# Attention's key and query reorderings cut into pieces of 512 columns, and two buffers of the last input restore moved

## The chip, the cores and the metric

The program runs on one core of one Trainium2 chip. What is measured is the device time of one execution in microseconds, here the median of three runs. A profile comes from one more execution, taken by the hardware profiler.

## The reference

One layer of a hybrid block on 2048 tokens of width 1024. The input x is normalised (RMSNorm) and multiplied by one matrix of 9216 columns, nine slices of 1024: for branch A u, v and a gate; for branch B queries, keys, values and a gate; and two merge gates.

Branch A applies gelu to u and v, normalises v, mixes the positions of each chunk of 128 tokens with a lower-triangular 128x128 matrix for each of 8 channel groups, and multiplies by u and by the SiLU of its gate.

Branch B is causal attention with 16 heads of 64 channels in three patterns of distance (dilations 1, 4 and 16; pattern numbers p = 0, 1, 2). In the pattern of dilation d a query sees up to 129 keys whose positions differ by multiples of d, with a penalty linear in distance:

```python
s = jnp.einsum('bhrnqd,bhrnkd->bhrnqk', qb, kw) * (Dh ** -0.5)
s = s - slopes[None, :, None, None, None, None] * (dist * dilation).astype(jnp.float32)
```

The three outputs are combined by their softmax denominators and multiplied by the SiLU of the gate of B. Then merged = g_a * (y_a @ w_proj_a) + g_b * (y_b @ w_proj_b), x + merged @ w_out, and a last RMSNorm.

## The kernel before

Matrix products that need float32 accuracy are made of three products of rounded parts (`mm3`, line 97): a matrix is split into a high part and the rest (`split_w`, `split_X`), and hi*hi, hi*lo and lo*hi are summed. A product of 128x1024 by 1024x512 is so 24 matmuls of 512 columns.

**First part, two halves of the sequence.** Each half has two quarters of 512 tokens (qd). `make_h` loads the transposed input, scales it by the norm's statistics `rsbc` (made in `stats`, line 155, held in pool `tp`) and splits it into tiles X. Most slices are multiplied with a seven-product scheme (`unit_S`, `unit_SR`, one level of Strassen), whose sums of quarters stand in the tiles T1, T2, T3 (pool `tp`) and T4. T4 takes the place of the first four chunks of the second quarter's X. So at the end of each half `restore` (line 216) loads these four chunks again, scales them with `rsbc` (line 151, on VectorE) and splits them (lines 144 and 145). It does this through the buffers of tag `ld`, of which there are three.

**Stage change.** When the second half ends, pools `tp`, `wr` and `cp` are closed, and what opens then, `wp` (weight blocks of 128 columns: `wraw`, `whi`, `wlo`) and `at` (everything of the attention), lies in the same memory. A tile of the new pools can be written only when the old tiles in its bytes have been read for the last time.

**Window (lines 747 to 825).** The attention of 16 heads runs as 192 groups (head, pattern in the order 2, 1, 0, group g of 4 blocks of 128 queries). Step j issues the scores of group j (`stage_s`), the transposes of the probabilities of group j-2 (`stage_t`), and the weighted sum of group j-3 (`stage_o`); in between, dense products (`fill`: the rest of the gates for the second half, then the projection of branch A) are put in by a fixed ratio, 8 matmuls at a time. The order on TensorE is that of the program text (`issue_after`); on the other engines, and in the DMA queue of SyncE, a scheduler orders instructions at compile time, and can put one that is ready ahead of earlier ones in the text.

**Reordering.** For patterns 1 and 2 the keys (a high part KH and a low part KL, fp16, 2048 columns) are copied into block order (`permute`, line 594), for pattern 2 the queries as well. Per head these are five copies of 128x2048: for pattern 2 QP on ScalarE, KHP and KLP on VectorE; for pattern 1 KHP on VectorE and KLP on ScalarE. In the text, the generator `permuted` is started at group 0 of the pattern ahead, and advanced one copy per step (line 803). QP has one buffer; KHP and KLP have two, which patterns 2 and 1 use in turn.

**Last part** (`final`): projection of branch B, merge, output projection, norm.

Of the kernel before, what the change touches and what calls it, by code (L numbers as in the profile page):

```python
# [9 lines left out]
F32 = mybir.dt.float32  # L10
F32R = mybir.dt.float32r
F16 = mybir.dt.float16
AF = mybir.ActivationFunctionType
ALU = mybir.AluOpType
AX = mybir.AxisListType

P = 128
D = 1024
T = 2048
KC = D // P  # L20
# [7 lines left out]
class Prog:  # L28
# [126 lines left out]
    def stats(self, hp, qd):  # L155
        nc, io = self.nc, self.io
        ss = hp.tile([P, 4], F32, name="ss", tag="ss")
        for b in range(4):
            xr = hp.tile([P, D], F32, name="xr", tag="xr", bufs=2)
            t0 = 512 * qd + P * b  # L160
            nc.sync.dma_start(out=xr, in_=io["x"][t0:t0 + P])
            nc.scalar.activation(xr, xr, AF.Square, accum_out=ss[:, b:b + 1])
        rs = hp.tile([P, 4], F32, name="rs", tag="rs")
        self.rsqrt_mean(rs, ss, 4)
        ps = self.pt()
        for i in range(4):
            nc.tensor.matmul(ps[:, i * P:(i + 1) * P], rs[:, i:i + 1].broadcast_to([P, P]), self.ident,
                             start=True, stop=True)
        bc = self.tp.tile([P, 512], F32, name="rsbc", tag=f"rsbc{qd % 2}")
        nc.scalar.copy(bc, ps)  # L170
        self.bc[qd % 2] = bc

# [43 lines left out]
    def restore(self, X, qd, ks=range(4)):  # L216

        for k in ks:
            X[1][k] = [self.xp.tile([P, 512], F32R, name=f"X1_{k}_{p}", tag=f"X1_{k}_{p}") for p in range(2)]
            self.split_X(X[1], k, self.h_chunk(self.wk, "ld", 3, qd, k))  # L220

    def wraw(self, w, c0):
        raw = self.wr.tile([P, KC, 256], F32, name="wraw2", tag="wraw2", bufs=2)
        self.nc.sync.dma_start(out=raw, in_=w[:, c0:c0 + 256].rearrange("(k p) n -> p k n", p=P))
        return raw
# [242 lines left out]

    def ev_av(self, hf):
        nc = self.nc  # L470
        self.ssv = self.tp.tile([P, 8, 4], F32, name="ssv", tag="ssv")

        def ev(wb, np_, ps):
            t = ps.rearrange("p (c n) -> p c n", c=2)
            nc.scalar.activation(t, t, AF.Gelu_apprx_tanh)
            j = self.wk.tile([P, 512], F32, name="junk", tag="t5")[:, :256]
            for c in range(2):
                n = 2 * np_ + c
                nc.scalar.activation(j, t[:, c], AF.Square, accum_out=self.ssv[:, n, wb:wb + 1])
            nc.sync.dma_start(out=self.av_d[hf][256 * np_:256 * np_ + 256, wb * 256:wb * 256 + 256]  # L480
                              .rearrange("(c p) d -> p c d", c=2), in_=t)
        return ev
# [111 lines left out]
    def permute(self, at, copy, t, name, p, bufs):  # L594

        r = at.tile([P, T], F16, name=name, tag=name, bufs=bufs)
        if p == 1:
            copy(r.rearrange("p (q n a) -> p q n a", q=4, n=4), t.rearrange("p (n a q) -> p q n a", q=4, n=4))
        else:
            copy(r.rearrange("p (q a) -> p q a", q=16), t.rearrange("p (a q) -> p q a", q=16))  # L600
        return r

    def permuted(self, at, raw, p):

        nc = self.nc
        Q, KH, KL = raw[:3]
        k = [Q.rearrange("p (n a q) -> p q n a", q=4, n=4)]
        if p == 2:
            k[0] = self.permute(at, nc.scalar.copy, Q, "QP", p, 1).rearrange("p (b a) -> p b a", a=P)
            yield  # L610
        k.append(self.permute(at, nc.vector.tensor_copy, KH, "KHP", p, 2))
        yield
        k.append(self.permute(at, nc.vector.tensor_copy if p == 2 else nc.scalar.copy, KL, "KLP", p, 2))
        self.qkp[p] = k

    def stage_s(self, at, G):
# [130 lines left out]
    def window(self, at, fill, total_fill):  # L747

        groups = []
        for h in range(NH):  # L750
            for p in (2, 1, 0):
                for g in range(4):
                    groups.append(dict(h=h, p=p, g=g))
        pend = []
        vt = {}
        self.qkp = {}
        perm = iter(())
        att_total = (0.109 * 2 + 0.088) * 75 * NH + 8 * 4 * 0.45
        state = dict(att=0.0, fill=0.0)
        ahead, behind = 6, 2  # L760
        ratio = (total_fill - (ahead + behind) * 5.2) / att_total

        def run(gen, keep=False):
            c = self.seg(gen)
            if c is None:
                return None
            state["att"] += c
            while state["fill"] < state["att"] * ratio:
                if self.seg(fill) is None:
                    break  # L770
                state["fill"] += 0.217 * self.every
            return c

        for _ in range(24 // self.every * 2):
            self.seg(fill)
        raw = {0: self.load_qk(at, 0)}
        for _ in self.permuted(at, raw[0], 2):
            pass
        vt[0, 2] = self.load_v(at, 0, 2)
        for _ in range(24 // self.every * (ahead - 2)):  # L780
            self.seg(fill)
        n = len(groups)
        for j in range(n + 3):
            if j < n:
                G = groups[j]
                h, p, g = G["h"], G["p"], G["g"]
                if g == 3 and j + 1 < n:
                    q = j // 4 + 1
                    vt[q // 3, 2 - q % 3] = self.load_v(at, q // 3, 2 - q % 3)
                if g == 0:  # L790
                    if p == 2:
                        OC = at.tile([P, 3, 16, 66], F32, name="OC", tag="OC", bufs=1)
                    if p == 1 and h + 1 < NH:
                        raw[h + 1] = self.load_qk(at, h + 1)
                if g == 0:
                    O = OC[:, 0] if p == 0 else at.tile([P, 16, 66], F32, name="ob", tag="ob", bufs=2)
                G.update(qk=self.qkp[p] if p else raw[h][:3], B=raw[h][3], V=vt[h, p], OC=OC, O=O)
                run(self.stage_s(at, G))

                nxt = {2: (h, 1), 0: (h + 1, 2)}.get(p)  # L800
                if nxt and nxt[0] < NH and g == 0:
                    perm = self.permuted(at, raw[nxt[0]], nxt[1])
                next(perm, None)
            if 2 <= j < n + 2:
                run(self.stage_t(at, groups[j - 2]))
            if j >= 3:
                G = groups[j - 3]
                run(self.stage_o(at, G))
                if G["p"] == 0 and G["g"] == 3:
                    pend.append(self.combine(at, G["h"], G["OC"]))  # L810
            if pend:
                if run(pend[0]) is None:
                    pend.pop(0)
            if j == n - 6:
                self.Y0 = self.alloc_X(0)
                self.load_Y(self.Y0, 0, range(7))
        for gen in pend:
            for _ in range(6):
                self.seg(gen)
            for _ in range(24 // self.every):  # L820
                self.seg(fill)
            while self.seg(gen) is not None:
                pass
        while self.seg(fill) is not None:
            pass
# [83 lines left out]
    def run(self):  # L909
# [5 lines left out]
        def drain(g):  # L915
            for _ in g:
                pass
        self.bc = [None, None]

        def pool(name, **kw):  # L920
            return tc.tile_pool(name=name, **kw)
        with pool("tp", bufs=1) as self.tp, pool("wr", bufs=2) as self.wr, pool("cp", bufs=1) as self.cp:
            X = [None, None]
            for hf in range(2):
                qds = (2 * hf, 2 * hf + 1)
                with pool(f"hp{hf}", bufs=2) as hp:
# [8 lines left out]
                    else:  # L935
# [4 lines left out]
                        X = [X0, [None] * KC]  # L940
# [17 lines left out]
                if hf == 0:  # L958
                    drain(self.unit_S(X, win, 6144, self.ev_bg, qds))
                    drain(self.unit_S(X, win, 7168, self.ev_gate(self.ga_d), qds))  # L960
                self.restore(X, qds[1])
        self.wp = self.ctx.enter_context(pool("wp", bufs=2))
        self.every = 8
        self.w_hi = self.nc.gpsimd
# [65 lines left out]
```

## Time and profile before

| | |
|---|---|
| median of 3 runs | 2685.8 us (2683.05 to 2686.45) |
| profiled execution | 2690.79 us, span 2688.8 us |
| TensorE busy | 2503.2 us (93%) |
| VectorE busy | 1794.8 us (67%) |
| ScalarE busy | 1255.1 us (47%) |
| GpSimd busy | 888.2 us (33%) |
| mean granted TensorE clock | 0.974 of full speed |

The span is the time from the first to the last instruction. In rows, times are in microseconds unless marked ns; PE is TensorE's matmul, PEld its weight load, DVE VectorE, ACT ScalarE, POOL GpSimd, SP SyncE; L103 is line 103 of the kernel. Busy matmuls overlap in the record, so that a busy share of PE near 100% says only that it was not waiting.

### The profile page before, as it was taken

What the parts mean: (1) busy time and instruction counts of PE and PEld (TensorE: products, weight loads), DVE (VectorE), ACT (ScalarE), POOL (GpSimd) and SP (SyncE); (2) the same over time, 40 slices, a digit from 0 to 9 for tenths busy, and PEclk for the clock granted to TensorE, in tenths of its full rate; (3) what the DMA queues carried; (4) which work ended last, traced back from release to release, by engine and by line L of the source; (5) the groups of instructions that cost most, each with busy time, mean ns of one, the idle gap of its engine ahead of it and who ended that gap; (6) DMA issues with size and microseconds to landing.
All of it is one profiled execution on the core that took longest, in us unless ns stands there. A gap on an engine that the chain in (4) does not pass through costs nothing.

```text
span 2688.8 us, 45128 instructions
## 1 busy us (share of the span) xinstructions
PE 2503.2 (93%) x16736; PEld 2122.7 (79%) x16736; DVE 1794.8 (67%) x3633; ACT 1255.1 (47%) x2481; POOL 888.2 (33%) x633
## 2 busy tenths in 40 slices
PE   5969999999998999999899899989889898899998
PEld 5969888888887898888677778878777777677787
DVE  5864767756258547677457877787989888545533
ACT  4335333343333353333257777676767665222221
POOL 0325554444444444544222222333333333000000
PEclk9989999999999999999899999999999999999999
DMA  7744333253453343323356646677777876755541
GB/s 232 162 126 142 102 118 106 94 171 116 153 167 89 87 138 115 122 95 114 99 142 158 185 127 181 177 195 201 200 217 194 237 206 176 239 168 184 169 132 63
DMA packets 463995, 410.00 MB, mean 152 GB/s; under 512 B 150432, under 2 KB 384288, under 8 KB 463776
## 3 DMA queue, kind: packets, MB, share of 16 engines
q1 hardware_dynamic: 463344, 407.05, 51.7%
q8 instruction: 132, 2.16, 0.3%
q14 instruction: 87, 0.71, 0.1%
q10 hardware_dynamic: 432, 0.07, 0.0%
HBM read 297.35 MB, written 109.71 MB: 151 GB/s over the span
## 4 chain that ended last, share of the span: by engine, by line
PE 67%; DVE 13%; DMA 10%; issue 4%; ACT 3%; POOL 1%; SPq 0%; ACTq 0%; DVEq 0%; POOLq 0%
PE pj L103 32%; PE pt L103 15%; PE ss L103 10%; PE pt L669 3%; DVE S L647 2%; PE ss L639 2%; DVE pl L673 1%; DVE X L145 1%; PE ss L640 1%; DMA v_d<-vst 1%; DMA wraw<-in_w_in 1%; DMA OC<-o_d 1%; DMA o_d<-ob 1%; PE pt L512 1%; DVE OC L727 1%
## 5 line engine op out<-in xcount | busy, mean ns | idle before, releaser
L103 PE MATMUL pj<-X,whi 128*128 128x512 f32 x1792 | 602.3, 411 | 16.5 <-POOL whi L85 11.1
L86 POOL TENSOR_TENSOR wc<-wraw,wc 128x512 fp32r<-128x512 f32 x240 | 327.4, 1372 | 318.7 <-ACT wc L83 307.2
L103 PEld LDWEIGHTS pj<-X,whi 128*128 128x128 f32 x1792 | 342.5, 195 | 88.1 <-POOL whi L85 12.0
L103 PE MATMUL pj<-X,wlo 128*128 128x512 f32 x896 | 369.2, 412 | 7.6 <-DVE wlo L86 4.0
L647 DVE CUSTOM_DVE_ANT_0 S<-ss,B,niqk 128x256 f32<-128x256 f32 (+1 forms) x768 | 284.3, 418 | 22.0 <-PE ss L640 21.8
L673 DVE SCALAR_TENSOR_TENSOR pl<-pt,ph 128x512 f16<-128x512 f32 x320 | 204.8, 653 | 93.3 <-ACT ph L672 92.0
L653 ACT ACTIVATE S<-S,ob 128x128 f32<-128x128 f32 (+1 forms) x512 | 193.4, 437 | 72.5 <-DVE ob L647 71.5
L83 ACT CAST wc<-wraw 128x512 fp32r<-128x512 f32 x240 | 145.2, 618 | 165.3 <-PE pt L103 78.8
L85 POOL TENSOR_SCALAR whi<-wraw 128x1024 fp32r<-128x1024 f32 x64 | 69.9, 1093 | 442.9 <-PE pj L103 393.2
L103 PEld LDWEIGHTS pj<-X,wlo 128*128 128x128 f32 x896 | 175.1, 195 | 46.5 <-DVE wlo L86 6.9
L672 ACT ACTIVATE ph<-pt 128x512 f16<-128x512 f32 x320 | 177.2, 565 | 61.1 <-PE pt L669 37.0
L103 PE MATMUL ss<-T,wc 128*128 128x512 f32 x768 | 188.2, 394 | 0.0
L103 PE MATMUL pt<-X,wc 128*128 128x512 f32 x768 | 185.2, 390 | 0.0
L103 PE MATMUL pj<-WO,X 128*128 128x512 f32 x768 | 180.7, 395 | 4.1 <-ACT X L872 3.9
L103 PEld LDWEIGHTS pj<-WO,X 128*128 128x128 f32 x768 | 144.2, 188 | 40.0 <-ACT X L872 5.2
L669 PE MATMUL pt<-ident,S 128*128 128x128 f32 x1200 | 168.6, 278 | 3.4 <-DVE pl L673 3.3
L86 POOL TENSOR_TENSOR wcl<-wraw,wch 128x1024 fp32r<-128x1024 f32 x52 | 129.2, 2486 | 121.4 <-ACT wch L83 97.2
L103 PEld LDWEIGHTS ss<-T,wc 128*128 128x128 f32 x768 | 143.6, 188 | 32.0
L103 PEld LDWEIGHTS pt<-X,wc 128*128 128x128 f32 x768 | 143.9, 188 | 30.3
L86 POOL TENSOR_TENSOR wlo<-wraw,whi 128x1024 fp32r<-128x1024 f32 x64 | 164.5, 2571 | 5.3
L103 PE MATMUL pt<-T,wc 128*128 128x512 f32 x672 | 165.0, 394 | 0.0
L669 PEld LDWEIGHTS pt<-ident,S 128*128 128x128 f32 x1200 | 141.7, 144 | 15.1 <-DVE pl L673 4.4
(229 smaller groups left out, 5777.8 us busy)
## 6 DMA issues: line engine op xcount, KB each, us to landing
wraw<-in_w_in SPq DMA_DIRECT2D x64, 1024.0 KB, 5.7
V<-v_d SPq DMA_DIRECT2D x48, 520.0 KB, 4.8
o_d<-ob SPq DMA_DIRECT2D x32, 528.0 KB, 5.1
OC<-o_d SPq DMA_DIRECT2D x32, 528.0 KB, 4.7
wraw<-in_w_in SPq DMA_DIRECT2D x32, 512.0 KB, 5.4
wraw<-in_w_proj_a SPq DMA_DIRECT2D x32, 512.0 KB, 5.3
wraw<-in_w_proj_b SPq DMA_DIRECT2D x32, 512.0 KB, 4.7
xt<-in_xT SPq DMA_DIRECT2D x60, 256.0 KB, 4.3
```

The source lines that it names most:

```text
L83: nc.scalar.copy(hi, raw)
L85: nc.gpsimd.tensor_scalar(out=hi, in0=raw, scalar1=1.0, scalar2=0.0, op0=ALU.mult, op1=ALU.add)
L86: self.w_lo.tensor_tensor(out=lo, in0=raw, in1=hi.bitcast(F32), op=ALU.subtract)
L103: self.pe = nc.tensor.matmul(out, st(a, k), mv(b, k), start=first and n == 0, stop=last and n == len(todo) - 1)
L145: self.x_lo.tensor_tensor(out=X[k][1], in0=src, in1=X[k][0].bitcast(F32), op=ALU.subtract)
L512: nc.tensor.matmul(px[:, i * P:(i + 1) * P], av[:, 4 * q + i], w, start=True, stop=True)
L639: nc.tensor.matmul(ps[:, i, :n], q, KH[:, w], start=True, stop=False)
L647: nc.vector.tensor_tensor_reduce(out=S[:, j, :n], in0=ps[:, i, :n], in1=B[:, bo:bo + n], scale=self.niqk[:, pr:pr + 1], scalar=3e38, op0=A ...
L653: nc.scalar.activation(S[:, i, :rng[i]], S[:, i, :rng[i]], AF.Exp, bias=ob[:, i, 65:66], scale=-1.0)
L669: self.pe = nc.tensor.transpose(px[:, j * P:(j + 1) * P], G["S"][:, i, c * P:(c + 1) * P], self.ident)
L672: nc.scalar.activation(ph[:, :n], px[:, :n], AF.Copy, scale=PSCALE)
L673: nc.vector.scalar_tensor_tensor(out=pl[:, :n], in0=px[:, :n], scalar=PSCALE, in1=ph[:, :n], op0=ALU.mult, op1=ALU.subtract)
```

## The change

`permute` makes four copies of 512 columns in place of one of 2048 (for pattern 1 one residue of the dilation each, for pattern 2 four residues each) and is now a generator that pauses after each. The window advances it at three places of a step, and empties it at the last group of a pattern. `rsbc` and `ssv` are allocated in pool `cp` in place of `tp`. The last restore is a new function: its four loads go into one 8 KB tile (per partition) of the ring `wraw2` in pool `wr`, not into the three buffers `ld`, and are scaled there in place.

```diff
@@ stats
-        bc = self.tp.tile([P, 512], F32, name="rsbc", tag=f"rsbc{qd % 2}")
+        bc = self.cp.tile([P, 512], F32, name="rsbc", tag=f"rsbc{qd % 2}")
@@ new
+    def restore_last(self, X, qd):
+        nc = self.nc
+        t = self.wr.tile([P, KC, 256], F32, name="xt4", tag="wraw2", bufs=2).rearrange("p (k a) n -> p k (a n)", k=4)
+        for k in range(4):
+            nc.sync.dma_start(out=t[:, k], in_=self.io["xT"][k * P:(k + 1) * P, qd * 512:qd * 512 + 512])
+        for k in range(4):
+            X[1][k] = [self.xp.tile([P, 512], F32R, name=f"X1_{k}_{p}", tag=f"X1_{k}_{p}") for p in range(2)]
+            nc.vector.scalar_tensor_tensor(out=t[:, k], in0=t[:, k], scalar=self.gn[:, k:k + 1], in1=self.bc[qd % 2],
+                                           op0=ALU.mult, op1=ALU.mult)
+            self.split_X(X[1], k, t[:, k])
@@ ev_av
-        self.ssv = self.tp.tile([P, 8, 4], F32, name="ssv", tag="ssv")
+        self.ssv = self.cp.tile([P, 8, 4], F32, name="ssv", tag="ssv")
@@ permute
-        if p == 1:
-            copy(r.rearrange("p (q n a) -> p q n a", q=4, n=4), t.rearrange("p (n a q) -> p q n a", q=4, n=4))
-        else:
-            copy(r.rearrange("p (q a) -> p q a", q=16), t.rearrange("p (a q) -> p q a", q=16))
+        for g in range(4):
+            if p == 1:
+                copy(r.rearrange("p (q n a) -> p q n a", q=4, n=4)[:, g],
+                     t.rearrange("p (n a q) -> p q n a", q=4, n=4)[:, g])
+            else:
+                copy(r.rearrange("p (q a) -> p q a", q=16)[:, 4 * g:4 * g + 4],
+                     t.rearrange("p (a q) -> p q a", q=16)[:, 4 * g:4 * g + 4])
+            yield
@@ permuted: each permute is now entered with "yield from"
@@ window, within step j
                 next(perm, None)
             if 2 <= j < n + 2:
                 run(self.stage_t(at, groups[j - 2]))
+            next(perm, None)
             if j >= 3:
                 G = groups[j - 3]
                 run(self.stage_o(at, G))
                 if G["p"] == 0 and G["g"] == 3:
                     pend.append(self.combine(at, G["h"], G["OC"]))
+            next(perm, None)
+            if j < n and groups[j]["g"] == 3:
+                for _ in perm:
+                    pass
@@ run
-                self.restore(X, qds[1])
+                (self.restore if hf == 0 else self.restore_last)(X, qds[1])
```

## Rows read from the trace of the kernel before

**Rows 1.** Busy time of each engine in stretches; columns as the first row says.
```profile
core 0: us, PE busy (x) PEld busy (x) DVE busy (x) ACT busy (x) POOL busy (x), PEclk, DMA share, GB/s
1340.00:2260.00 920.00, 840.25 (x8036) 704.68 (x8035) 744.47 (x2233) 630.96 (x1384) 283.60 (x195) 0.97 0.68 187
```
**Rows 2.** Timeline of the stage change: start, duration, engine, instruction, [idle before <-releaser].
```profile
1305.51 2.96 PE L103 MATMUL pt<-T,wc 128*128 128x512 f32 x12
...
1316.10 0.33 SPq L150 DMA_DIRECT2D xt<-in_xT  x1
...
1319.56 0.75 DVE L151 SCALAR_TENSOR_TENSOR xt<-xt,gn,rsbc 128x512 f32<-128x512 f32 x1 [0.48 <-DMA xt<-in_xT]
...
1320.37 0.38 SPq L91 DMA_DIRECT2D wraw<-in_w_in  x1
1321.66 0.32 SPq L524 DMA_DIRECT2D ya_d<-tg  x1
...
1325.21 1.05 POOL L85 TENSOR_SCALAR whi<-wraw 128x1024 fp32r<-128x1024 f32 x1 [30.25 <-DMA wraw<-in_w_in]
1326.31 1.22 PE L103 MATMUL pj<-X,whi 128*128 128x512 f32 x2 [9.58 <-POOL whi L85]
1328.74 0.79 PE L103 MATMUL pj<-X,wlo 128*128 128x512 f32 x1 [1.21 <-POOL wlo L86]
...
1335.96 0.60 ACT L543 ACTIVATE tbg<-pj 128x512 f32<-128x512 f32 x1 [0.80 <-PE pj L103]
```
**Rows 3.** The first dense product of the window, columns as in Rows 1.
```profile
1326.31:1335.90 9.59, 8.38 (x25) 6.22 (x26) 2.19 (x1) 4.19 (x1) 3.15 (x2) 0.67 0.88 208
```
**Rows 4.** The copies: line, engine, count, minimum/median/maximum ns, first and last start.
```profile
L598 ACT COPY KLP<-KL x16: 2059/2082/2117, 1336.5 to 2191.8; 128x2048 f16<-128x2048 f16 x16
L600 ACT COPY QP<-Q x16: 4114/4172/4247, 1331.0 to 2171.2; 128x2048 f16<-128x2048 f16 x16
L600 DVE COPY KHP<-KH x16: 1984/2122/4057, 1332.4 to 2174.5; 128x2048 f16<-128x2048 f16 x16
```
**Rows 5.** Timeline of ScalarE, VectorE and TensorE around 1705 us.
```profile
1701.00 4.14 ACT L600 COPY QP<-Q 128x2048 f16<-128x2048 f16 x1
...
1704.37 2.14 DVE L600 COPY KHP<-KH 128x2048 f16<-128x2048 f16 x1
1706.21 0.58 ACT L672 ACTIVATE ph<-pt 128x512 f16<-128x512 f32 x1
1706.54 2.07 DVE L600 COPY KLP<-KL 128x2048 f16<-128x2048 f16 x1
...
1708.52 0.69 DVE L673 SCALAR_TENSOR_TENSOR pl<-pt,ph 128x512 f16<-128x512 f32 x1
...
1709.26 0.20 PE L688 MATMUL po<-V,pl 128*128 128x65 f16 x1 [1.93 <-DVE pl L673]
```
**Rows 6.** 16 us from each QP copy, heads 1 to 15; columns of Rows 1.
```profile
1425.02:1441.02 16.00, 12.74 (x102) 10.65 (x101) 15.36 (x44) 11.96 (x22) 3.77 (x4) 0.89 0.32 103
...
1536.26:1552.26 16.00, 11.23 (x75) 8.91 (x75) 16.00 (x37) 10.91 (x19) 7.68 (x5) 0.79 0.41 129
...
sum 240.00, PE 191.93 PEld 156.22 DVE 231.90 ACT 180.79 POOL 82.55; mean PE 12.79 PEld 10.41 DVE 15.46 ACT 12.05 POOL 5.50
```
**Rows 7.** Groups by line and shape: count, busy us, mean ns, idle before.
```profile
L83 ACT CAST wc<-wraw 128x512 fp32r<-128x512 f32 x240 | 145.2, 618 | 165.3 <-PE pt L103 78.8 <-PE pj L103 50.3 <-PE ss L103 30.6
L83 ACT CAST wch<-wraw 128x1024 fp32r<-128x1024 f32 x60 | 62.3, 1042 | 64.4 <-DMA wraw<-in_w_in 27.2 <-PE pt L103 15.2 <-issue 11.6
L363 DVE TENSOR_TENSOR u<-pt,u 128x512 f32<-128x512 f32 x80 | 54.7, 683 | 19.8 <-PE pt L103 19.8
L86 DVE TENSOR_TENSOR wlo<-wraw,whi 128x1024 fp32r<-128x1024 f32 x32 | 39.0, 1219 | 9.3 <-ACT whi L83 9.3
L653 ACT ACTIVATE S<-S,ob 128x128 f32<-128x128 f32 x320 | 108.6, 396 | 70.2 <-DVE ob L647 69.5
```
**Rows 8.** Timeline of ScalarE: four exponentials of 128 columns in a row.
```profile
1748.11 1.28 ACT L653 ACTIVATE S<-S,ob 128x128 f32<-128x128 f32 x4
```

More of the change, by code (lines that the diff above doesn't have):

```diff
@@ L608, in permuted @@
         if p == 2:
[L609 to L613, printed above, removed]
+            r = yield from self.permute(at, nc.scalar.copy, Q, "QP", p, 1)
+            k[0] = r.rearrange("p (b a) -> p b a", a=P)
+        k.append((yield from self.permute(at, nc.vector.tensor_copy, KH, "KHP", p, 2)))
+        k.append((yield from self.permute(at, nc.vector.tensor_copy if p == 2 else nc.scalar.copy, KL, "KLP", p, 2)))
         self.qkp[p] = k
```

## The prediction, made before the changed kernel ran

> **What bounds the kernel now.** I first read the busy time by stretches. In the window of the attention, 920 us long, TensorE is busy 840.25 us and VectorE 744.47 (81%); TensorE is granted 0.97 of its clock [rows 1]. So TensorE bounds the window, but 79.8 us of it are idle, and the missing 0.03 of the clock is worth some 27 us more. Next I read the timeline where TensorE stands still longest, the change from the second half to the window. Its row of the first matmul there says 9.58 us idle, released by GpSimd's split of the first weight block [rows 2]. Then I looked for what is near the idle time inside the window. The 16 us after each query copy of heads 1 to 15, 240 us together, hold 48.1 of the 79.8 idle microseconds (240 - 191.93), and VectorE is busy 231.90 of them, 97% [rows 6]. The reader is to see one stall per head, always behind the same copies, and one long stall at the stage change.
>
> **The stage change: rsbc to another pool, four input chunks through another buffer.** TensorE's last product of the half ends at 1326.31 - 9.58 = 1316.73 [rows 2]. The load of the first weight block is issued at 1320.37, 0.06 us after the scaling of line 151 ends (1319.56 + 0.75), which is the last reader of rsbc; so that block lies on rsbc's bytes. That scaling waited for the fourth chunk, whose load could be issued only at 1316.10, when the first of three buffers came free. From the load's issue to GpSimd's start are 4.84 us, then 1.05 us for the high part, then the matmul, and another 1.21 us for the low part [rows 2].
>
> With rsbc in `cp`, pool `tp` begins with T1, so the first weight block lies on T1, whose last product ends at 1305.51 + 2.96 = 1308.47 [rows 2]. Issued then, the load lets GpSimd start at 1313.3, the high part is there at 1314.4, before TensorE needs it at 1316.7. I leave 0.3 us for the low part. The four chunks no longer wait for one another, and are scaled before T4 is free; only the splits come after it. They are for the second quarter's chunks, used one dense product later.
>
> [...] Its 24 matmuls end at 1335.9 (ScalarE's evacuation starts at 1335.96 [rows 2]), 19.2 us after 1316.73. At the pace of the product before (2.96 us for 12 [rows 2]) they take 5.9 us, with the 0.3 us 6.2. So 13.0 us go. Both ends: if the weight load is queued on SyncE behind the last store of the half, now issued at 1321.66 [rows 2], it comes 1.6 us later than today, a loss of 1.6; the most is 13.0. I take 13.0, since today's queue already lets the load pass that store. Nothing is added: the four loads and scalings (0.75 us each [rows 2]) are as many as before, and if no idle VectorE time covered them at the earlier place they would cost 3.0 us. The buffers of the attention that lie on the new staging tile must wait for its last split, near 1319; the query copy that began at 1331.0 [rows 4] has six dense products of some 5.9 us before its first reader, so nothing waits. What is late next is the second weight block, whose load follows the first evacuation in SyncE's queue; I leave that as it is. Moving ssv costs nothing: it is read long before.
>
> **The copies in pieces.** Per head, 4.17 us on ScalarE (QP) and about 2.1 us twice on VectorE (KHP, KLP) for pattern 2, 2.08 us on ScalarE for pattern 1 [rows 4], and one more KHP. QP has one buffer, and KHP and KLP get theirs back at the same moment, the end of pattern 2's scores, so all three are let go together. At 1701 the trace shows what follows: ScalarE is held for 4.14 us, its next eviction runs at 1706.21; VectorE has meanwhile begun KHP at 1704.37 and goes on with KLP, so the low part `pl` of that eviction starts at 1708.52 only, and TensorE waits 1.93 us for it [rows 5]. Over 15 heads 48.1 us of idle time, 3.2 each. The clock adds to this: of the 15 stretches five have 0.89, three 0.79, one 0.80 and six 1.00 ([rows 6] has one of each of the first two); 16 times the shortfall (5 x 0.11 + 3 x 0.21 + 0.20) is 22.1 us. It fell after the idle stretches; part of it overlaps them. Up to 70 us could go.
>
> After the change the longest hold is one piece: on ScalarE 4.17 / 4 plus a fixed part, 1.1 to 1.2 us; on VectorE 2.12 / 4 plus a fixed part, 0.6 to 0.7 us, and an exponential or a `pl` that is ready can go in between. But the work stays, and VectorE has only 8.1 us of 240 free there [rows 6]. The idle time goes only where pieces spread past these 16 us, into a window in which VectorE is idle 19% and ScalarE 31% [rows 1]. That the code advances the copies at three places of a step doesn't settle this: the order is the compile-time scheduler's. Bounds: from 0 gone (pieces back to back) to all 70. The row nearest is the one stall in detail: 4.1 us of copies in a row on VectorE give a wait of 1.93 us, so a hold of up to about 2 us passes unseen, and two pieces in a row are below that. I take half of the idle time, 24 us, and 13 of the 22 us of clock: 37 us.
>
> The price is 15 more instructions per head, 9 on VectorE and 6 on ScalarE. A ScalarE cast takes 618 ns for 512 columns and 1042 for 1024, so 194 ns are fixed; VectorE's 683 and 1219 leave 147 [rows 7]. In a row they overlap: four exponentials of 396 ns each [rows 7] take 1.28 us together [rows 8], 0.295 apart, so about 0.1 of it is hidden. I take 0.1 us each, 16 x 15 x 0.1 = 24 us on two engines, hidden in the idle shares above: 0 on the path. If that cover is gone it is at most 16 x (9 x 0.147 + 6 x 0.194) = 40 us.
>
> [...]
>
> **Sum.** 13.0 + 37 = 50 us off the profiled execution of 2690.8 (span 2688.8 plus 2.0 around it) gives 2640.8. That execution was 5.0 us above the median of the runs, 2685.8, so I predict 2636.
>
> **Rivals.**
> Pieces back to back: all are let go at one moment and an engine that looks idle to the scheduler takes them all. For it: KHP and KLP follow each other within 0.03 us at 1706.5 [rows 5]; against it: the stall's chain had other work ready in between. Then only the 13 us go, and 6 more VectorE pieces x 0.1 x 15 = 9 us may land in a full stretch: 2673 to 2682. Chance 0.15.
> Slower: the fixed cost of the pieces lands on the chain from exponential to eviction to `pl`. Place: the 16 us behind each pattern 2, where the 9 us added on VectorE exceed the 8.1 free; from that point on every added microsecond delays TensorE. With nothing of the stall gone and all 40 us on the path, 13 gained: 2713; with half of it landing 2693. For it: the 97% [rows 6]. Against it: ScalarE is busy 75% there (180.79 of 240), and the copies have two patterns' time until they are read. Chance 0.11.
> The stage change does not move, the weight load being queued behind the stores, while the pieces work: 2685.8 + 1.6 - 37 = 2650. Chance 0.10.
> Gain and price cancel, within 0.2% (5.4 us, about what a measurement of this kernel can tell from no change): 0.07.
>
> **How the numbers follow.** My forecast has 0.57, between 2605 (83 us, all of 13 and 70) and 2665. Faster by over 0.2%: 0.57 + 0.10 + 0.15 = 0.82; within: 0.07; slower: 0.11. The range leaves out the last two cases and a little at the low end, where all idle time would have to go: 2609 to 2678.
>
> **What would show it.** In the profile after: the first weight load of the window issued before TensorE's last product of the half ends, no idle time above 1 us before its first matmul, and a granted clock of 1.00 there. In the window, the copies as 16 x 4 per kind, near 1.1 us on ScalarE and 0.6 on VectorE, with exponentials between them; fewer of the once-per-head waits for `pl` and for the score reduction; a clock nearer 1. The prediction is wrong if the idle time of the 15 places stays near 3 us each with the pieces in a row, if VectorE's waits for ScalarE grow, or if new waits for loads take the place of the old ones.

## The result, and the profile after

The changed kernel takes 2655.99 us (median, 2653.71 to 2664.80) beside 2686.12 of the kernel before: ratio 0.9896, 95% interval 0.9871 to 0.9921, or 30.1 us less. Timed once more beside the experiments it gave 2657.75 against 2690.23, ratio 0.9882 [0.9856, 0.9908], 32.5 us less. The forecast was 2636, with a range that held the result: the direction and one term were right, the other term was too large by 17 us. Differences in this document are between medians; the ratios weigh all executions, so the two can lie some us apart.

The profiled execution after took 2664.8 us (span 2663.0, granted clock 0.982); the one before 2690.8. Between the end of the half's last product and the first scores lie 38.6 us (1323.50 to 1362.14) where 52.2 were (1316.73 to 1368.96); from the first scores to those of the last head 828.1 (to 2190.22) where 848.2 were (to 2217.14). So 13.6 and 20.1 us went; 6.8 came back because in this one execution the products ahead ended later, which the ten other profiled executions with the same first part do not show (1314 to 1320).

The window, to be read against [rows 1]: idle time fell from 79.8 to 71.5 us, the clock rose from 0.97 to 0.99, and VectorE is 48 us busier in the same 920 us.

```profile
1340.00:2260.00 920.00, 848.53 (x8258) 711.04 (x8256) 792.28 (x2423) 656.41 (x1510) 283.59 (x197) 0.99 0.69 191
```

The stage change, timeline after, to be read against [rows 2]:

```profile
1312.31 2.88 PE L103 MATMUL pt<-T,wc 128*128 128x512 f32 x12
1315.03 2.88 PE L103 MATMUL ss<-T,wc 128*128 128x512 f32 x12
...
1317.94 1.01 SPq L91 DMA_DIRECT2D wraw<-in_w_in  x2
...
1322.07 1.05 POOL L85 TENSOR_SCALAR whi<-wraw 128x1024 fp32r<-128x1024 f32 x1 [20.41 <-DMA wraw<-in_w_in]
...
1323.20 2.66 POOL L86 TENSOR_TENSOR wlo<-wraw,whi 128x1024 fp32r<-128x1024 f32 x1
1323.34 0.62 PE L103 MATMUL pj<-X,whi 128*128 128x512 f32 x2
1323.57 2.83 DVE L534 SCALAR_TENSOR_TENSOR tg<-tg,u 128x512 f32<-128x512 f32 x1
...
1325.91 0.67 PE L103 MATMUL pj<-X,wlo 128*128 128x512 f32 x1 [1.95 <-POOL wlo L86]
```

The first matmul of the window starts without idle time. The weight load goes out when the product after T1's has ended (1317.94 against 1315.03 + 2.88 = 1317.91), so TensorE waits 1.95 us for the low part. Over a stretch as long as that of [rows 3] the granted clock is 0.82, where it was 0.67:

```profile
1323.34:1332.93 9.59, 7.64 (x27) 5.78 (x27) 9.59 (x8) 1.45 (x3) 6.66 (x3) 0.82 0.33 98
```

The 16 us from the first piece of each query copy, heads 1 to 15 (against [rows 6]; one of the two stretches at 0.89, and the sum): TensorE stands still for 240 - 208.21 = 31.8 us, not 48.1, and the clock's shortfall is 16 x (2 x 0.11 + 0.02) = 3.8, not 22.1. VectorE is as full as before.

```profile
1524.04:1540.04 16.00, 12.42 (x101) 10.49 (x101) 16.00 (x45) 11.95 (x24) 6.93 (x6) 0.89 0.44 131
...
sum 240.00, PE 208.21 PEld 171.62 DVE 231.47 ACT 205.38 POOL 100.22; mean PE 13.88 PEld 11.44 DVE 15.43 ACT 13.69 POOL 6.68
```

The pieces, by line (columns of [rows 4]); the maxima of 2603 to 2894 ns are VectorE pieces that started beside a GpSimd instruction (last section):

```profile
L614 ACT COPY QP<-Q x64: 1105/1184/1282, 1343.4 to 2152.8; 128x512 f16<-128x512 f16 x64
L614 DVE COPY KHP<-KH x64: 534/655/2692, 1344.5 to 2170.1; 128x512 f16<-128x512 f16 x64
L614 DVE COPY KLP<-KL x64: 601/654/2894, 1349.6 to 2178.2; 128x512 f16<-128x512 f16 x64
...
L611 DVE COPY KHP<-KH x64: 404/420/2603, 1347.0 to 2180.8; 128x512 f16<-128x512 f16 x64
L611 ACT COPY KLP<-KL x64: 634/669/697, 1348.5 to 2172.8; 128x512 f16<-128x512 f16 x64
```

TensorE's waits in 1340 to 2260, before and after (total us, times, longest). The waits of the scores for the score reduction (L639 before, L654 after) became more numerous and shorter, those of the weighted sum for `pl` (L688, L703) fewer and half as long in sum, and the transposes (L669, L684), which need a PSUM buffer that `pl` has read, have a wait that they had three times before and now 14 times.

```profile
PE ss L639 <- DVE ob L647: 38.7, 59, 4.3
PE po L688 <- DVE pl L673: 18.4, 17, 3.0
PE po L686 <- ACT ob L689: 11.3, 12, 1.4
...
PE pt L669 <- DVE pl L673: 3.3, 3, 2.9
PE pj L103 <- POOL wlo L86: 2.5, 2, 1.7
PE pj L103 <- POOL whi L85: 1.5, 1, 1.5
```

```profile
PE ss L654 <- DVE ob L662: 35.1, 72, 2.6
PE pt L684 <- DVE pl L688: 14.0, 14, 2.9
PE po L703 <- DVE pl L688: 9.2, 13, 2.6
PE po L701 <- ACT ob L704: 6.6, 10, 1.8
```

What such a wait looks like after the change (timeline around 1709 us):

```profile
1709.03 2.41 POOL L86 TENSOR_TENSOR wlo<-wraw,whi 128x1024 fp32r<-128x1024 f32 x1
1709.29 4.27 DVE L614 COPY KLP<-KL 128x512 f16<-128x512 f16 x4
...
1710.62 0.48 ACT L687 ACTIVATE ph<-pt 128x384 f16<-128x384 f32 x1
...
1713.45 0.44 DVE L611 COPY KHP<-KH 128x512 f16<-128x512 f16 x1
1713.79 0.57 DVE L688 SCALAR_TENSOR_TENSOR pl<-pt,ph 128x384 f16<-128x384 f32 x1
...
1714.41 0.55 PE L684 MATMUL pt<-ident,S 128*128 128x128 f32 x3 [2.08 <-DVE pl L688]
```

The eviction `ph` is done at 1711.10, but its low part `pl` stands in VectorE's order behind four pieces of KLP and one of KHP, which hold VectorE for 4.5 us, where the two whole copies of [rows 5] took 4.2. The first of the four alone takes 2.66 us of this, because it starts beside GpSimd's subtraction; the other three follow each other 0.53 to 0.54 us apart. So pieces do run back to back. Counted over the whole window, of VectorE's 192 pieces 59 stand alone, 30 in pairs and 103 in rows of three to seven; of the 64 pieces of QP on ScalarE 32 stand alone, 22 in pairs and 10 in rows of three or four, and with ScalarE's KLP pieces counted in, as on VectorE, 49, 34 and 45 of 128. In time: copies held ScalarE for more than 2 us without a break 32 times before, 100 us together, and 19 times after, 48 us; VectorE 33 times, 78 us, and 23 times, 71 us. ScalarE's copies were broken up, VectorE's mostly moved: at most heads two or three KHP pieces run at the release, the rest 20 us later or more, among the copies of pattern 1.

### The profile page after: what moved, and what is told of

The parts are those of the page before. It is cut to its first block, busy times and chain, and to the rows that moved or that the text cites. A ratio compares the mean times of both kernels' runs of the same rounds, so it can differ in the third digit from the quotient of the medians.

```text
span 2663.0 us, 45389 instructions
## 1 busy us (share of the span) xinstructions
PE 2497.5 (94%) x16736; PEld 2112.4 (79%) x16736; DVE 1835.0 (69%) x3777; ACT 1261.1 (47%) x2577; POOL 886.1 (33%) x633
## 3 DMA queue, kind: packets, MB, share of 16 engines
q1 hardware_dynamic: 463344, 407.05, 52.2%
## 5 line engine op out<-in xcount | busy, mean ns | idle before, releaser
L86 POOL TENSOR_TENSOR wc<-wraw,wc 128x512 fp32r<-128x512 f32 x240 | 327.5, 1373 | 322.7 <-ACT wc L83 316.1
L688 DVE SCALAR_TENSOR_TENSOR pl<-pt,ph 128x512 f16<-128x512 f32 x320 | 204.8, 652 | 74.4 <-ACT ph L687 73.5
L687 ACT ACTIVATE ph<-pt 128x512 f16<-128x512 f32 x320 | 176.5, 563 | 47.3 <-PE pt L684 28.5
L684 PE MATMUL pt<-ident,S 128*128 128x128 f32 x1200 | 168.4, 276 | 14.1 <-DVE pl L688 14.0
L86 POOL TENSOR_TENSOR wcl<-wraw,wch 128x1024 fp32r<-128x1024 f32 x52 | 129.2, 2486 | 124.6 <-ACT wch L83 103.6
L86 POOL TENSOR_TENSOR wlo<-wraw,whi 128x1024 fp32r<-128x1024 f32 x64 | 163.1, 2548 | 5.3
L684 PEld LDWEIGHTS pt<-ident,S 128*128 128x128 f32 x1200 | 138.9, 142 | 28.7 <-DVE pl L688 18.3
```

Source lines behind the costliest of these rows:

```text
L86: self.w_lo.tensor_tensor(out=lo, in0=raw, in1=hi.bitcast(F32), op=ALU.subtract)
L684: self.pe = nc.tensor.transpose(px[:, j * P:(j + 1) * P], G["S"][:, i, c * P:(c + 1) * P], self.ident)
L687: nc.scalar.activation(ph[:, :n], px[:, :n], AF.Copy, scale=PSCALE)
L688: nc.vector.scalar_tensor_tensor(out=pl[:, :n], in0=px[:, :n], scalar=PSCALE, in1=ph[:, :n], op0=ALU.mult, op1=ALU.subtract)
```

## The experiments

Times are medians; each difference is to the kernel before, run beside on the same chip. The first four runs, the next four and the last four are three such groups, so runs of different groups are compared by their differences.

**One part alone.** The first run has only the two buffer changes (the first three hunks of the diff and the last), the second only the pieces.

```diff
# e1_buffers_only: permute, permuted and the window as before
# e2_pieces_only
-        bc = self.cp.tile(...)
+        bc = self.tp.tile(...)
... (ssv likewise; restore_last is left out)
-                (self.restore if hf == 0 else self.restore_last)(X, qds[1])
+                self.restore(X, qds[1])
```

> The buffer changes alone (rsbc and ssv in cp, the last restore through its own tile); the copies whole as before. Theory A (the change is a sum of two parts, each seen in the trace): from the end of the half's last product to the first score of the window the trace of after needs 38.7 us, that of before 52.2, so this kernel should be about 13 us faster than before, near 2673, with the window as before (about 848 us from the first scores to those of the last head). Theory B (the part ahead of the stage change, 6.7 us later in the profile after, is a cost of the new placement of tiles): only 5 to 7 us faster, 2680, and the late 6.7 us show in this profile too. Theory C (the stage change's gain is given back in the window): no change, 2686.

> The copies in pieces alone, buffers as before. Theory A: the window from first scores to those of the last head falls from 848 to about 828 us, so 17 to 20 us faster than before, near 2668; the 9.6 us of idle time at the stage change stay. Theory C (all of the gain comes from the stage change, the pieces' extra VectorE time of 45 us eats theirs): no change, 2686 or slower.

Buffers only: 2677.71 against 2690.69, 0.9938 [0.9920, 0.9957], 13.0 us less. Pieces only: 2670.45, 0.9917 [0.9896, 0.9937], 20.2 us less. Together 33.2; the whole change had 30.1 and 32.5. Within the intervals, 5 to 7 us to either side, the parts add up, so neither hides the other. The timelines of the stage change (buffers only, then pieces only) show that only the first part moves the weight load ahead of the matmul that needs it:

```profile
1309.81 1.01 SPq L91 DMA_DIRECT2D wraw<-in_w_in  x2
...
1313.82 1.05 POOL L85 TENSOR_SCALAR whi<-wraw 128x1024 fp32r<-128x1024 f32 x1 [20.30 <-DMA wraw<-in_w_in]
...
1315.20 0.63 PE L103 MATMUL pj<-X,whi 128*128 128x512 f32 x2
1317.67 0.50 PE L103 MATMUL pj<-X,wlo 128*128 128x512 f32 x1 [1.84 <-POOL wlo L86]
```

```profile
1317.53 0.38 SPq L91 DMA_DIRECT2D wraw<-in_w_in  x1
...
1324.63 1.22 PE L103 MATMUL pj<-X,whi 128*128 128x512 f32 x2 [10.87 <-POOL whi L85]
```

**Pieces on one engine**, with the buffer changes. The first has pieces on ScalarE and whole copies on VectorE, the second the reverse.

```diff
# permute, e3_scalar_pieces (e4_vector_pieces: the same line without "not")
+        if not (name == "QP" or (name == "KLP" and p == 1)):
+            copy(<the whole tile, as before>)
+            yield
+            return r
```

> The changed kernel, but only the ScalarE copies (QP of pattern 2, KLP of pattern 1) in pieces; the three VectorE copies are whole. Theory A1 (the hold of ScalarE by QP, 4.2 us, is what stalls TensorE; VectorE pieces mostly cost): VectorE's 45 us of extra time go, and the time is equal to the changed kernel or up to 10 us less, 2646 to 2656. Theory A2 (the double hold of VectorE by KHP and KLP is what stalls): most of the window's 20 us is lost, 2668 to 2674.

> The changed kernel, but only the VectorE copies in pieces; QP and the KLP of pattern 1 are whole on ScalarE. Theory A1: most of the window's 20 us is lost, 2668 to 2676. Theory A2: near the changed kernel, 2655 to 2660.

ScalarE's pieces: 2660.78 against 2690.69, 0.9891 [0.9874, 0.9909], 29.9 us less: nearly the whole change. VectorE's: 2672.14, 0.9915 [0.9892, 0.9939], 18.6 less, only 5.6 more than the buffers alone. So by the medians most of the gain of the pieces comes from ScalarE's two copies (QP, and KLP of pattern 1, which this run does not tell apart). TensorE's waits for ScalarE's eviction of the weighted sum, whose one PSUM buffer the next sum needs, fall by 9.6 us with them (buffers only, then with ScalarE's pieces):

```profile
PE po L698 <- ACT ob L701: 13.7, 14, 1.5
PE po L708 <- ACT ob L711: 4.1, 9, 1.2
```

But this gain lies only in part where the prediction looked for it. The 15 stretches of 16 us, as in [rows 6], in the two runs (ScalarE's pieces, then VectorE's), and the same for each kernel's profile:

```profile
sum 240.00, PE 197.84 PEld 161.69 DVE 235.14 ACT 191.88 POOL 86.57; mean PE 13.19 PEld 10.78 DVE 15.68 ACT 12.79 POOL 5.77
sum 240.00, PE 207.32 PEld 170.63 DVE 229.34 ACT 199.83 POOL 99.76; mean PE 13.82 PEld 11.38 DVE 15.29 ACT 13.32 POOL 6.65
```

| us | TensorE idle in the 15 stretches | clock's shortfall there | idle in the rest of 1340 to 2260 | first scores to those of the last head | median less than before |
|---|---|---|---|---|---|
| before | 48.1 | 22.1 | 31.7 | 848.2 | |
| buffers only | 50.6 | 18.6 | 31.7 | 852.7 | 13.0 |
| buffers, ScalarE's pieces | 42.2 | 18.7 | 31.6 | 836.2 | 29.9 |
| buffers, VectorE's pieces | 32.7 | 5.3 | 47.3 | 842.9 | 18.6 |
| the change | 31.8 | 3.8 | 39.7 | 828.1 | 30.1 |

It is VectorE's pieces that empty the 15 stretches and raise the clock there, and they give most of it back as idle time elsewhere. ScalarE's pieces take 8.4 us of idle time out of them, leave the clock there as it was, and bring the larger gain. Two profiled executions of one kernel differ by some us in the fifth column (828.1 and 825.0 for the change), so a share of 10 us for VectorE's pieces, which that column would give, is not excluded by the 5.6 and 2.6 of the medians.

**The changed kernel again, and the copies taken away.** The second keeps the copies of head 0 alone and uses them for every head; it shows what the copies still cost.

```diff
# permuted, e5_no_copies
+        old = self.qkp.get(p)
+        if old is not None:
+            self.qkp[p] = (... Q in place ... if p == 1 else old[:1]) + old[1:]
+            return
```

> The changed kernel once more, beside the next three. The two parts alone gave 13 and 20 us. Theory A (they add): about 33 us faster than before, ratio 0.987 to 0.989. The products ahead of the stage change ended at 1323.4 us in its first profile and at 1315 to 1318 in three kernels with the same first part; if that was one execution's scatter, here they end near 1316 again and the span is some 5 us shorter than 2663.

> Upper bound: the reorder copies are made for head 0 only; heads 1 to 15 score patterns 1 and 2 against head 0's reordered keys (and, in pattern 2, its queries), so that part of the computation is left out. Theory A (what is left of the window's idle time still comes from the copies, about 130 us of VectorE and 115 of ScalarE): another 20 to 35 us off the changed kernel, near 2625, VectorE's share of the window down by 14 points. Theory D (the copies no longer matter; the rest comes from the score reduction, the evictions and the combine): within 8 us of the changed kernel.

The changed kernel took 2657.75; in its second profile the products ahead of the stage change end at 1317.0, so the 6.8 us of the first were that execution's. Without copies: 2608.58 against 2690.23, 0.9696 [0.9672, 0.9720], 81.7 us less, so 49 below the changed kernel, more than either theory had. Less the 13.0 of the buffers, the copies cost the kernel before 69 us, and the pieces get back 20 of them. Window without copies:

```profile
1340.00:2260.00 920.00, 868.34 (x8412) 732.28 (x8411) 717.76 (x2278) 576.32 (x1404) 279.00 (x202) 0.99 0.73 204
```

**GpSimd's subtraction in four parts, and queries read in place.** VectorE pieces that take 2.7 us in place of 0.65 lie beside GpSimd's split of a weight block. The first run cuts that subtraction into four; the second has e3's form but lets TensorE read the queries of pattern 2 at a step of 16, without QP.

```diff
# split_w, e6_gpsimd_quarters
+        if self.w_hi is nc.gpsimd:
+            for i in range(4):
+                s = slice(2 * i, 2 * i + 2)
+                nc.gpsimd.tensor_tensor(out=lo[:, s], in0=raw[:, s], in1=hi[:, s].bitcast(F32), op=ALU.subtract)
+            return
# permuted, e7_queries_in_place
-            r = yield from self.permute(at, nc.scalar.copy, Q, "QP", p, 1)
-            k[0] = r.rearrange("p (b a) -> p b a", a=P)
+            k[0] = Q.rearrange("p (a b) -> p b a", b=16)
```

> The changed kernel with GpSimd's subtraction for a weight block's low part (2.4 us) made as four instructions, in the window only. In the trace 16 VectorE copies last 0.5 to 2.0 us longer than the others, 22 us together, and each ends with GpSimd's subtraction that was running; before the change there were 5 and 7 us. Theory E (VectorE copies wait for the GpSimd instruction in progress, and this wait comes on TensorE's path): the longest copy falls from 2.9 to about 1.3 us, the waits of the transposes for pl from 14 us to under 6, the time by 6 to 12 us. Theory F (the waits are hidden): the copies get shorter, the time does not change by more than 3 us.

> Only ScalarE's KLP in pieces, VectorE's copies whole, and no copy of the queries: TensorE loads them for pattern 2 at a step of 16 elements, as it does for pattern 1 at a step of 4 (107 ns a load there, 97 in block order). Theory A1 (the hold of ScalarE by the query copy is what stalled TensorE): 4.7 us of ScalarE per head go, and if the loads stay near 107 ns the time is 5 to 15 us below the kernel with ScalarE pieces. Theory G (the load slows with the step): 512 loads at 200 ns or more put 50 us or more on TensorE, slower than before.

In four parts: 2630.59 against 2690.23, 0.9794 [0.9768, 0.9820], 27 us below the changed kernel and more than expected. Queries in place: 2657.92, 0.9884 [0.9862, 0.9907], the same as with QP in pieces on ScalarE. Nothing is won by taking the ScalarE copy away altogether: the weight loads from Q at a step of 16 are slower (149 ns in this run; contiguous ones, those from QP among them, take 97 and those at a step of 4 take 114, where the 107 of the expectation was a mean of the last two), and the wait for VectorE's whole copies stays, up to 5.4 us at a time:

```profile
PE ss L660 <- DVE ob L668: 43.5, 55, 5.4
PE po L709 <- DVE pl L694: 14.4, 7, 4.6
```

**Does the gain of the four parts belong to this change?** The first of these is the kernel before with only GpSimd's cut; the second e3's form with the cut (whole copies on VectorE); the third cuts into eight.

```diff
# e8_before_quarters: before.split_w cut in four
# e9_whole_vector_quarters: e3's permute with e6's split_w
# e10_gpsimd_eighths (against e6)
-            for i in range(4):
-                s = slice(2 * i, 2 * i + 2)
+            for i in range(8):
+                s = slice(i, i + 1)
```

> The kernel before with only GpSimd's low-part subtraction of the window in four instructions (whole copies, old buffers). In the changed kernel the same edit took 17 to 27 us. Theory H (VectorE waits behind GpSimd whatever the size of its copies; the pieces have nothing to do with it): 15 us or more faster than before, 2675 or less. Theory E2 (the pieces made the waits: 16 of them with 22 us against 5 with 7): under 8 us faster, 2682 or more.

> ScalarE's copies in pieces, VectorE's whole, GpSimd's low part in quarters, the new buffers. Without the quarters, VectorE's pieces gained about 8 us in the window and nothing in the total. Theory E2 (pieces on VectorE are worth their price once GpSimd's instruction is short): 8 to 15 us slower than the changed kernel with quarters (2631), so 2639 to 2646. Theory I (whole copies are cheaper on VectorE, by 22 us of fixed parts): 2631 or less.

> The changed kernel with GpSimd's low part in eight instructions of 128 columns in place of four of 256. Theory E (what counts is how long one GpSimd instruction holds VectorE off): a further gain of 2 to 6 us over the quarters, VectorE's copies and two-input instructions a little shorter again. Theory J (the quarters gained by giving TensorE the low part's first chunks earlier): no change from quarters, since GpSimd's whole time for a block grows.

Against 2691.70: before with four parts 2666.30, 0.9909 [0.9894, 0.9924], 25.4 us less; whole VectorE copies with four parts 2647.09, 0.9851 [0.9829, 0.9873], 44.6 less; eight parts 2630.05, 0.9769 [0.9750, 0.9788], 61.7 less, as with four (59.6). So the cut is a gain of its own, as large without the pieces. With it the change is worth 59.6 - 25.4 = 34.2 us, without it 32.5: shortening the hold by GpSimd does not bring back the missing 17 us. What it seems to alter is the share of VectorE's pieces: 2.6 us without the cut (32.5 - 29.9), 15.0 with it (59.6 - 44.6), while the buffers and ScalarE's pieces are then worth 19.2 (44.6 - 25.4) in place of 29.9. The intervals of these runs are 4 to 7 us wide to either side, so the 15.0 are clear of zero, while the 2.6 are not and the difference of the two is just at its limit. The pieces stand in the same rows with the cut (59 alone, 30 in pairs, 103 in rows), but hold VectorE for more than 2 us only 17 times, 52 us, where it was 71. Groups by line in the window of the changed kernel, of four and of eight parts:

```profile
L86 POOL TENSOR_TENSOR wlo<-wraw,whi 128x1024 fp32r<-128x1024 f32 x61 | 155.3, 2546 | 5.1
...
L614 DVE COPY KLP<-KL 128x512 f16<-128x512 f16 x64 | 54.5, 903 | 0.0
L614 DVE COPY KHP<-KH 128x512 f16<-128x512 f16 x64 | 50.0, 797 | 4.7 <-DMA KH<-k_d 4.7
...
L611 DVE COPY KHP<-KH 128x512 f16<-128x512 f16 x64 | 29.7, 502 | 0.0
```

```profile
L89 POOL TENSOR_TENSOR wlo<-wraw,whi 128x256 fp32r<-128x256 f32 x244 | 209.0, 887 | 5.1
...
L619 DVE COPY KLP<-KL 128x512 f16<-128x512 f16 x64 | 44.5, 745 | 0.0
L619 DVE COPY KHP<-KH 128x512 f16<-128x512 f16 x60 | 44.1, 747 | 0.0
```

```profile
L89 POOL TENSOR_TENSOR wlo<-wraw,whi 128x128 fp32r<-128x128 f32 x488 | 249.2, 545 | 5.1
...
L619 DVE COPY KLP<-KL 128x512 f16<-128x512 f16 x64 | 44.1, 741 | 0.0
```

A block costs GpSimd 2.5 us whole, 3.5 in four and 4.4 in eight parts, out of its idle time; VectorE's pieces lose 0.16 us (KLP) from whole to four, and nothing more to eight.

**The places in the text.** One `yield` per copy, after its four pieces, and one place in a step, as in the kernel before.

```diff
# e11_one_place
         for g in range(4):
             ...
-            yield
+        yield
-            next(perm, None)   # both added places
```

> The changed kernel, but the four pieces of a copy are issued together, at the one place of a step where the whole copy was issued before. Theory K (the scheduler's order decides, the place in the text does not): the time of the changed kernel, 2650 to 2662. Theory L (the three places per step are what spreads the pieces): most of the window's 20 us is lost, 2668 or more.

2655.00 against 2691.70, 0.9870 [0.9852, 0.9888], 36.7 us less: no worse than the change. VectorE's pieces stand in the same rows (59, 30 and 103). The order in which the pieces run is the scheduler's, not that of the places in the text.

## Why the prediction was right, and where not

**The stage change, 13.0 us: right.** Alone it gives 13.0 by the medians (by the ratio 11.6 to 21.5). The 24 matmuls of the working are the window's first product: in the profile before, behind the 9.58 us of idle time, the granted clock was 0.50 from 1326.31 to 1332.00 and 0.91 from there to 1335.90, so more than the gap could go. Two details differ, and that they cancel is luck. The load goes out 2.7 us later than worked out, a product later, so the low part is 1.95 us late and not 0.3, with the clock at 0.82 and not 1.00 behind it: 1.65 and 1.7 us. In return the second weight block, left "as it is" in the working, is no longer late, because its load now goes out together with the first (x2 in the timeline): TensorE's waits for its high part, 1.5 us, and its low part, 1.7, are gone.

**The clock, 13 of 22 us: more than that.** 18 us of shortfall went from the 15 places, nearly all. But it was not worth its microseconds: with VectorE's pieces alone as much goes (5.3 left) and the median falls by 5.6 us beyond the buffers, with ScalarE's alone 18.7 stay and it falls by 16.9.

**Half of the idle time, 24 us: too much, and this is the step that failed.** In the 15 places 16.3 us went, and outside them idle time rose from 31.7 to 39.7, by 8.0. The prediction took it that the pieces spread, with at most two in a row, and that a hold of up to 2 us passes unseen. On ScalarE that mostly came out: 54 of 64 pieces of QP stand alone or in pairs, and half of the time in holds of more than 2 us is gone (100 to 48 us). On VectorE 103 of 192 stand in rows of three and more, 71 of 78 us in such holds stay, and the row at 1709 shows the old hold at a new place. The two one-engine runs fit this: pieces on ScalarE alone give 29.9 of 32.5 us. The rows are not the whole of it, since with GpSimd's cut the same rows are worth 15.0 us: of the 14 pieces held beside GpSimd's subtraction 12 are a hold of more than 2 us each, up to 2.89. The upper bound of 70 us was close (69 without copies); the share was 20 of it instead of 37.

**The price, 0 on the path: too low in sum.** On VectorE the nine pieces more per head were put at 0.1 us each, 13.5 us. The groups give, per head, 2.27 + 2.23 + 1.46 = 5.96 us before (34.0 and 33.5 over 15 copies, 23.3 over 16) and (54.5 + 50.0 + 29.7)/16 = 8.39 after: 39 us over 16 heads. Some 23 of these are pieces held beside GpSimd, a term that the working did not have (counting those more than 0.2 us over the median of their line, 22 pieces with 31.1 us, where an expectation above said 16 and 22; before, seven copies with 8.1). The rest, 16 us, is the fixed part, near the 13.5 taken: a piece takes 655 ns by the median where a quarter of 2122 is 530. In a row it overlaps, since those pieces start 0.53 to 0.54 us apart, so it counts less than it looks. ScalarE's six pieces more cost (4 x 1.184 - 4.172 + 4 x 0.669 - 2.082)/6 = 0.19 us each, the upper bound of the working, in time that it had.

**The rivals.** "Pieces back to back" held for more of VectorE's pieces than of ScalarE's, and the time lies between it (2673 to 2682) and the forecast. The slower case did not come: in the full 16 us VectorE does no more than before (231.47 of 240), because most of its pieces moved out of them. The stage change did move.

**Left open.** Why the scheduler puts VectorE's pieces in rows was not tried, nor QP's pieces without KLP's. Nor is it settled why the cut of GpSimd's subtraction is worth 25 us to the kernel before, where only 8.1 us of its copies were visibly held; other VectorE work fell too (the 768-column multiplication from 1062 to 1001 ns, 60 times, the combination `cb` from 681 to 612), but these do not make 25. That TensorE gets the first parts of a block's low part earlier, the theory that eight parts did not refute, cannot make it either: all its waits for `wlo` in that window are 2.5 us.

## What to carry to other kernels

Here cutting long copies paid on the engine that had free time, ScalarE (16.9 us beyond the buffers); on VectorE, 97% busy where the copies are released, the pieces came out in rows (103 of 192 in rows of three and more), most of the hold moved (71 of 78 us stayed in holds of more than 2 us), and by the medians VectorE's pieces brought 2.6 us, with GpSimd's cut 15.0. So count how many pieces stand in a row before counting on them. Idle time that leaves the stretch one looks at may come back outside it (16.3 us left the 15 places, 8.0 came back), so measure the whole window. Take the copies away once: that run shows how much they cost in all. Best here is the change together with GpSimd's subtraction in four parts, 59.6 us (ratio 0.9794) below the kernel before; eight parts are as good.

## What the runs showed of the hardware

A VectorE copy that starts beside a GpSimd instruction mostly lasts until 0.3 to 0.6 us after that one ends: so 22 of the 32 pieces that start beside one in the changed kernel. One more starts 0.04 us before GpSimd's end, and the other nine run at their usual length while GpSimd's instruction takes longer (six of them, in one row, beside a subtraction of 5.5 us). The timeline around 1526 us:

```profile
1525.27 1.07 POOL L85 TENSOR_SCALAR whi<-wraw 128x1024 fp32r<-128x1024 f32 x1 [0.22 <-PE pj L103]
1525.35 1.49 DVE L614 COPY KHP<-KH 128x512 f16<-128x512 f16 x1
...
1526.43 2.69 POOL L86 TENSOR_TENSOR wlo<-wraw,whi 128x1024 fp32r<-128x1024 f32 x1
...
1526.91 2.69 DVE L614 COPY KHP<-KH 128x512 f16<-128x512 f16 x1
```

The copies end at 1526.84 and 1529.60, GpSimd's instructions at 1526.34 and 1529.12; by the median such a piece takes 0.655 us. Of VectorE's instructions with two inputs, L534 was held alike in the stage change above: it lasts 2.83 us, from 1323.57 to 0.54 us behind the end of L86, where the one before it, at 1319.34, took 0.69. `pl` (L688), which has two inputs too, was not: over 512 columns it takes 0.691 us by the median where it starts beside L86 with more than 1 us of that still to run (24 times), and 0.686 elsewhere (216 times). What makes the one wait for the other, and why not always, no run here shows. A held piece lost 1.4 us in the mean (31.1/22) and a held copy 1.2 (8.1/7), so cutting the copies alone raised the loss (from 8.1 us in seven copies to 31.1 in 22 pieces), and cutting the instruction that holds them lowered it (15.9 in 29 pieces with four parts).
